# Wide matmuls of a unit ahead of its narrow ones, and values for two pairs of heads in wide matmuls

## The chip, the core and the metric

The kernel runs on one NeuronCore of a Trainium2 chip. What counts is the device time of one execution in microseconds. TensorE (PE) multiplies into PSUM; its weight loads are a row of their own (PEld) and overlap its matmuls. VectorE (DVE), ScalarE (ACT) and GpSimd (POOL) work on SBUF and, the first two, on PSUM; SyncE (SP) issues the DMAs. Each engine takes its instructions in order and waits for the others through semaphores.

## What is computed

Two decoder layers on 256 tokens of width 2048 in float32: latent attention and a convolutional feed-forward (FFN), then dilated attention in three groups and another FFN, each behind an RMS norm and with a residual. In short:

```python
def dilated_mixer(h, positions, w_in, wo):
    qkv = (h @ w_in).reshape(B, S, G, 3, DIL_HEADS, DIL_HEAD_DIM)      # G 3, 16 heads of 128
    for g, (window, dilation) in enumerate(DIL_GROUPS):
        q = partial_rope(qkv[:, :, g, 0], positions)
        k = partial_rope(qkv[:, :, g, 1], positions)
        v = qkv[:, :, g, 2]
        o, l = dilated_group_attention(q, k, v, window, dilation, DIL_HEAD_DIM ** -0.5)
    ...
def conv_ffn(h, w_up, conv_w, conv_b, w_down):                          # hidden 5632
    u = h @ w_up
    ...
    return (jax.nn.silu(gate) * val) @ w_down
def reference(...):
    for i in range(DEPTH):                                              # 2
        h = rms_norm(x, attn_norm[i])
        x = x + (mla_mixer if i % 2 == 0 else dilated_mixer)(h, ...)
        x = x + conv_ffn(rms_norm(x, ffn_norm[i]), ...)
    return rms_norm(x, final_norm)
```

## The kernel before

Activations stand as 16 blocks of 128 features by 256 tokens. Products are made to float32 accuracy from two parts of each factor: ACT copies a factor to the type fp32r (the high part, wh or the left half of xs) and DVE subtracts that copy (the low part, wl or the right half of xs). Three of the four part products count: high by high, high weight by low activation, low weight by high activation.

A **unit** is one output block of 128 features for all tokens. `load` (L68) brings 128 x 2048 weights (1 MB) into one of three staging tiles `w` and splits them, 1024 columns at a time, into wh and wl tiles, of which the pool `wsp` has five each; one unit takes two of each. `proj` (L105) then goes through the 16 blocks k of the sum (14 or 16 in the down projections). For each block it makes a **wide** matmul of 512 columns, wh with both parts of xs, into a whole PSUM bank, and a **narrow** one of 256 columns, wl with the high part, into the bank's right half. In the first block the wide one goes first, in all others the narrow one, so that they alternate:

```python
                def hi():
                    nc.tensor.matmul(ps, wh, xs[k], start=(k == 0), stop=(k == n - 1))

                def lo():
                    nc.tensor.matmul(ps[:, T:], wl, xs[k][:, :T], start=False, stop=False)
                for f in ((hi, lo) if k == 0 else (lo, hi)):
                    f()
```

`joined` (L181) adds the two halves of the bank afterwards: ACT copies the right one to `lo`, DVE adds the left one into `sum`. `unit` (L174) puts down the products of a unit, then one step of attention from the list `steps`, then the evacuation of the unit before; four PSUM banks (`pp`) rotate.

The stages are: the rank projection of the queries (L446 to L460, four banks at once, products as the weights come), the kv ranks, eight pairs of heads of latent attention with short units of 256-column matmuls (`mm3`, L99), the output projection, the first FFN, eight pairs of heads of dilated attention, its output projection, the second FFN, the final norm. An FFN has 88 up units (44 blocks, gate and value) and three down projections of 16 units over 14, 14 and 16 blocks. After an up unit DVE writes `upad`, ACT makes the convolution's first tap `cv` (L724) and DVE the other two (L727), then the gate's product and a split into `a`.

In the dilated stage each pair of heads has 12 units for q and k (three groups, two heads) and 6 for values: `proj_tok` (L123) has 128 tokens as rows and the 2 x 128 columns of a pair as columns, the weights streaming as the moving factor, wide ones with the high and narrow ones with the low part of the activations, alternating as above. `joined_tok` (L189) joins the halves with the norm's factor, and group 0 is split again. Attention's steps of a pair (scores and softmax, two turnings of the probabilities, values, for each of two heads) lie between the units of the next pair.

A scheduler orders each engine's instructions; it may move work between units where its data allow it. The pools set how far: a tile's next writer waits for its last reader.

## Time and profile before

| | us |
|---|---|
| median of 3 runs (2743.19 to 2743.86) | 2743.84 |
| profiled execution, its own time | 2743.58 |
| its span, from first to last instruction | 2741.8 |

| engine | busy us | share of the span | instructions |
|---|---|---|---|
| PE | 2721.1 | 99% | 15964 |
| PEld | 2385.6 | 87% | 15964 |
| DVE | 2016.4 | 74% | 3553 |
| ACT | 1458.2 | 53% | 2305 |
| POOL | 21.5 | 1% | 39 |

Busy time counts a matmul from its start to a modelled end, and matmuls overlap, so PE's share tells that it always has one under way, not how fast they go. For that one reads the distance between starts, which the chain of work prints as the length of its pieces. DMA moves 180 GB/s on average. PE's granted clock stands at nine tenths or more in all 40 slices of the page.

### The profile page before, as it was taken

The page shows a single profiled execution, that of the slowest core. Times are in us where ns is not written, and L with a number is a line of the kernel's source. Part 1 is how long each engine was busy: PE and PEld are TensorE (multiplying, and loading weights), DVE is VectorE, ACT ScalarE, POOL GpSimd, SP SyncE. Part 2 cuts the span into 40 slices and gives each one's busy share as a digit, 9 for nine tenths or more (in the row PEclk, how much of TensorE's full clock was granted, in tenths as well). Part 3 has the DMA queues.
Part 4 walks back from the last instruction along what each step waited for, and adds up shares of the span by engine and source line. Part 5 has one row for each costly group of instructions (what it writes and reads, how often), then busy time and mean ns, then how long its engine had stood idle before and what let it go on. Part 6 is the DMA issues. An engine that isn't in the chain of part 4 may idle for free.

```text
span 2741.8 us, 40682 instructions
## 1 busy us (share of the span) xinstructions
PE 2721.1 (99%) x15964; PEld 2385.6 (87%) x15964; DVE 2016.4 (74%) x3553; ACT 1458.2 (53%) x2305; POOL 21.5 (1%) x39
## 2 busy tenths in 40 slices
PE   8999999999999999999999999999999999999998
PEld 7998888888888888888888888888888888888887
DVE  7987787677678767767767767676778768767775
ACT  6775655455455554545445445454565545545553
POOL 2000000000000000000000000000000000000000
PEclk9999999999999999999999999999999999999999
DMA  6345555555555555454554454544555555555553
GB/s 240 136 142 196 183 189 173 196 185 183 187 198 185 192 185 186 168 185 156 183 185 164 174 174 164 187 158 167 199 184 185 181 192 190 183 185 192 186 187 119
DMA packets 72191, 493.63 MB, mean 180 GB/s; under 512 B 8128, under 2 KB 9280, under 8 KB 21184
## 3 DMA queue, kind: packets, MB, share of 16 engines
q1 hardware_dynamic: 72000, 491.04, 51.8%
q8 instruction: 125, 2.05, 0.3%
q14 instruction: 66, 0.54, 0.1%
HBM read 488.91 MB, written 2.10 MB: 179 GB/s over the span
## 4 chain that ended last, share of the span: by engine, by line
PE 71%; issue 27%; DVE 1%; DMA 0%; ACT 0%; SPq 0%; POOLq 0%; POOL 0%; DVEq 0%; ACTq 0%
PE pp L115 36%; PE pp L118 18%; PE pp L131 7%; PE pp L134 3%; PE pp L101 1%; PE pp L103 1%; PE pp L102 1%; PE po L686 1%; PE ps L655 1%; PE pt L666 1%; DVE xs L233 0%; DMA w<-in_wqa 0%; PE ps L101 0%; PE ps L102 0%; PE ps L103 0%
## 5 line engine op out<-in xcount | busy, mean ns | idle before, releaser
L115 PE MATMUL pp<-xs,wh 128*128 128x512 f32 x4432 | 1554.6, 398 | 0.0
L89 DVE TENSOR_TENSOR wl<-w,wh 128x1024 fp32r<-128x1024 f32 (+2 forms) x843 | 1010.2, 1199 | 318.4 <-ACT wh L88 304.7
L118 PE MATMUL pp<-xs,wl 128*128 128x256 f32 x4432 | 1198.7, 281 | 0.0
L88 ACT ACTIVATE wh<-w 128x1024 fp32r<-128x1024 f32 (+2 forms) x843 | 874.1, 1037 | 604.5 <-PE pp L115 568.5
L115 PEld LDWEIGHTS pp<-xs,wh 128*128 128x128 f32 x4432 | 818.4, 188 | 180.3
L118 PEld LDWEIGHTS pp<-xs,wl 128*128 128x128 f32 x4432 | 837.2, 189 | 22.2
L115 PE MATMUL pp<-a,wh 128*128 128x512 f32 x1920 | 667.9, 397 | 0.0
L118 PE MATMUL pp<-a,wl 128*128 128x256 f32 x1920 | 516.7, 280 | 0.0
L115 PEld LDWEIGHTS pp<-a,wh 128*128 128x128 f32 x1920 | 352.4, 188 | 75.9
L118 PEld LDWEIGHTS pp<-a,wl 128*128 128x128 f32 x1920 | 362.3, 189 | 10.9
L184 ACT ACTIVATE lo<-pp 128x256 f32<-128x256 f32 x273 | 104.1, 381 | 325.9 <-PE pp L115 325.8
L186 DVE TENSOR_TENSOR sum<-pp,lo 128x256 f32<-128x256 f32 x273 | 115.5, 423 | 184.7 <-ACT lo L184 184.7
L727 DVE SCALAR_TENSOR_TENSOR cv<-upad,convs,cv 128x256 f32<-128x256 f32 x352 | 169.1, 482 | 6.1
L131 PE MATMUL pp<-wh,xs 128*128 128x512 f32 x384 | 146.9, 400 | 0.0
L131 PE MATMUL pp<-wl,xs 128*128 128x512 f32 x384 | 144.2, 398 | 0.0
L333 DVE TENSOR_TENSOR x<-x,pp 128x256 f32<-128x256 f32 x256 | 106.8, 420 | 50.7 <-PE pp L115 46.7
L94 ACT ACTIVATE wl<-w 128x512 fp32r<-128x512 f32 x104 | 65.7, 632 | 127.3 <-PE pp L118 127.3
L134 PE MATMUL pp<-wl,xs 128*128 128x256 f32 x384 | 107.8, 281 | 0.0
L724 ACT ACTIVATE cv<-upad,convs 128x256 f32<-128x256 f32 x176 | 105.8, 602 | 0.9 <-DVE upad L721 0.7
L95 DVE TENSOR_TENSOR wl<-w,wl 128x512 fp32r<-128x512 f32 x104 | 71.7, 690 | 42.8 <-ACT wl L94 40.6
L134 PE MATMUL pp<-wh,xs 128*128 128x256 f32 x384 | 99.7, 280 | 0.0
L131 PEld LDWEIGHTS pp<-wl,xs 128*128 128x128 f32 x384 | 72.1, 188 | 17.8
(208 smaller groups left out, 2025.1 us busy)
## 6 DMA issues: line engine op xcount, KB each, us to landing
w<-in_wup SPq DMA_DIRECT2D x176, 1024.0 KB, 4.7
w<-in_win SPq DMA_DIRECT2D x144, 1024.0 KB, 4.8
w<-in_wdn SPq DMA_DIRECT2D x64, 896.0 KB, 4.5
w<-in_wdn SPq DMA_DIRECT2D x32, 1024.0 KB, 4.8
w<-in_wo SPq DMA_DIRECT2D x16, 1024.0 KB, 4.8
w<-in_dwo SPq DMA_DIRECT2D x16, 1024.0 KB, 4.7
w<-in_wkvb SPq DMA_DIRECT2D x8, 1024.0 KB, 4.8
w<-in_wqb SPq DMA_DIRECT2D x8, 768.0 KB, 4.2
```

The costliest lines, as they stand in the source:

```text
L88: nc.scalar.activation(h, w[:, c:e], AF.Copy)
L89: nc.vector.tensor_sub(l, w[:, c:e], h.bitcast(F32))
L95: nc.vector.tensor_sub(t4[:, :, 1, :], src2, t4[:, :, 0, :].bitcast(F32))
L115: nc.tensor.matmul(ps, wh, xs[k], start=(k == 0), stop=(k == n - 1))
L118: nc.tensor.matmul(ps[:, T:], wl, xs[k][:, :T], start=False, stop=False)
L131: nc.tensor.matmul(ps, xs[k][:, tt * P:(tt + 1) * P], w, start=(k == 0), stop=(k == n - 1))
L134: nc.tensor.matmul(ps[:, T:], xs[k][:, T + tt * P:T + (tt + 1) * P], w[:, :T], start=False, stop=False)
L184: nc.scalar.activation(t, ps[:, T:], AF.Copy)
L186: nc.vector.tensor_add(u, ps[:, :T], t)
L333: nc.vector.tensor_add(x, x, a)
L724: nc.scalar.activation(c, u[:, 2:], AF.Identity, scale=convs[:, cw + 2:cw + 3], bias=convs[:, cw + 3:cw + 4])
L727: nc.vector.scalar_tensor_tensor(c, u[:, j:j + T], convs[:, cw + j:cw + j + 1], c, op0=ALU.mult, op1=ALU.add)
```

## The change

- `proj` puts down all wide matmuls of a unit first and then all its narrow ones, and the rank projection of the queries does the same for its four banks in each block.
- Values of the dilated stage are made for two pairs of heads at a time, in every second pair's turn. `load_tok2` brings a quarter of the sum (four blocks) for 2 x 256 columns in two DMAs of 512 KB and splits it so that the 512 columns of a block lie side by side. `proj_tok2` keeps two banks (128 tokens each) open over four quarters and makes all three part products as wide matmuls, added in the bank, so that nothing is left to be joined. Every such quarter is a unit; an even pair's turn has 24 units and an odd one's 12, instead of 18 each.
- `joined_tok` goes; `keep_v` makes one split of 512 columns in group 0 and one copy of 512 in the others, and the value tiles are twice as wide.
- To make room: tiles of `tmp` 4 for 5, of the q and k splits 4 for 5, of probabilities `p` 3 for 4, of `acc` and `sq` (squares for the norms) 1 for 2.
- The second head's scores come one step later.

```diff
-        work = ctx.enter_context(tc.tile_pool(name="work", bufs=5))
+        work = ctx.enter_context(tc.tile_pool(name="work", bufs=4))
...
-            for k in range(since, upto or n):
+            ks = range(since, upto or n)
+
+            def block(k, i):
                 a = k * P
-                wh, wl = (t[:, a % WS:a % WS + P] for t in w[a // WS])
-
-                def hi():
-                    nc.tensor.matmul(ps, wh, xs[k], start=(k == 0), stop=(k == n - 1))
-
-                def lo():
-                    nc.tensor.matmul(ps[:, T:], wl, xs[k][:, :T], start=False, stop=False)
-                for f in ((hi, lo) if k == 0 else (lo, hi)):
-                    f()
+                return w[a // WS][i][:, a % WS:a % WS + P]
+
+            for k in ks:
+                nc.tensor.matmul(ps, block(k, 0), xs[k], start=(k == 0), stop=(k == n - 1))
+            for k in ks:
+                nc.tensor.matmul(ps[:, T:], block(k, 1), xs[k][:, :T], start=False, stop=(k == n - 1),
+                                 skip_group_check=True)
             return ps
...
+        def load_tok2(srcs, q):
+            w = wst.tile([P, D], F32, name="w", tag="w")
+            for i, src in enumerate(srcs):
+                nc.sync.dma_start(w[:, i * WS:(i + 1) * WS], src[q // 2][:, q % 2 * WS:(q % 2 + 1) * WS])
+            w4 = w.rearrange("p (i k c) -> p i k c", i=2, c=T)
+            parts = []
+            for h in range(2):
+                wh = wsp.tile([P, WS], F32R, name="wh", tag="wh")
+                wl = wsp.tile([P, WS], F32R, name="wl", tag="wl")
+                wh4, wl4 = (t.rearrange("p (k i c) -> p i k c", i=2, c=T) for t in (wh, wl))
+                src = w4[:, :, 2 * h:2 * h + 2, :]
+                nc.scalar.activation(wh4, src, AF.Copy)
+                nc.vector.tensor_sub(wl4, src, wh4.bitcast(F32))
+                parts += [(wh[:, ts(k, 512)], wl[:, ts(k, 512)]) for k in range(2)]
+            return parts
+
+        def proj_tok2(w, pss_, xs, q):
+            for k4, (wh, wl) in enumerate(w):
+                k = 4 * q + k4
+                for tt, ps in enumerate(pss_):
+                    xh, xl = xs[k][:, ts(tt, P)], xs[k][:, T + tt * P:T + (tt + 1) * P]
+                    nc.tensor.matmul(ps, xh, wh, start=k == 0, stop=False)
+                    nc.tensor.matmul(ps, xl, wh, start=False, stop=False)
+                    nc.tensor.matmul(ps, xh, wl, start=False, stop=k == KC - 1)
...
-                acc = small.tile([P, T], F32, name="acc", tag="acc", bufs=2)
+                acc = small.tile([P, T], F32, name="acc", tag="acc", bufs=1)
...
-                sq = small.tile([P, T], F32, name="sq", tag="sq", bufs=2)
+                sq = small.tile([P, T], F32, name="sq", tag="sq", bufs=1)
...
-                        h[what] = att.tile([P, 2 * T], F32R, name="qks", tag="qks", bufs=5)
+                        h[what] = att.tile([P, 2 * T], F32R, name="qks", tag="qks", bufs=4)
...
-                        p = att.tile([P, 2 * T], F32, name="p", tag="p", bufs=4)
+                        p = att.tile([P, 2 * T], F32, name="p", tag="p", bufs=3)
...
+                if j % 2 == 0:
+                    state["v"] = {}
+                values = h["v"] = state["v"]
...
+                        if g == 0:
+                            v = att.tile([P, 4 * T], F32R, name="vs", tag="vs", bufs=2)
+                            split((v[:, :2 * T], v[:, 2 * T:]), ps, col)
+                        else:
+                            v = att.tile([P, 2 * T], F32, name="v", tag="v", bufs=4)
+                            nc.scalar.activation(v, ps, AF.Copy, scale=col)
...
+                    if j % 2 == 0:
+                        srcs = [(win_d[b + 4], win_d[b + 5]) for b in (base, base + 6 * NG)]
+                        pss_ = [pp.tile([P, 512], F32, name="pp", tag="pp") for _ in range(2)]
+                        for q in range(4):
+                            w = load_tok2(srcs, q)
+
+                            def quarter():
+                                proj_tok2(w, pss_, xs, q)
+                                return pss_
+
+                            unit(quarter, (lambda p, g=g: keep_v(g, p)) if q == 3 else (lambda p: None))
...
-                (s0, ta0, tb0, v0), (s1, ta1, tb1, v1) = attend(h, 0), attend(h, 1)
+                (s0, ta0, tb0, v0), (s1, ta1, tb1, v1) = (attend(h, e, (j % 2 * 2 + e) * P) for e in range(2))
-                steps.extend([s0, together(ta0, s1), tb0, together(v0, ta1), tb1, v1])
+                steps.extend([s0, ta0, together(tb0, s1), together(v0, ta1), tb1, v1])
```

The first place is PE at the seam of two units of the dilated stage (q or k). Before:

```order
L118 MATMUL pp<-xs_10510,wl 128x256
L115 MATMUL pp<-xs_10510,wh 128x512
L118 MATMUL pp<-xs_10518,wl 128x256
L115 MATMUL pp<-xs_10518,wh 128x512
L115 MATMUL pp<-xs_9795,wh 128x512
L118 MATMUL pp<-xs_9795,wl 128x256
L118 MATMUL pp<-xs_9804,wl 128x256
L115 MATMUL pp<-xs_9804,wh 128x512
```

Now, inside such a unit, where its wide matmuls end and its narrow ones begin:

```order
L117 MATMUL pp<-xs_10408,wh 128x512
L117 MATMUL pp<-xs_10459,wh 128x512
L117 MATMUL pp<-xs_10510,wh 128x512
L117 MATMUL pp<-xs_10518,wh 128x512
L119 MATMUL pp<-xs_9795,wl 128x256
L119 MATMUL pp<-xs_9804,wl 128x256
L119 MATMUL pp<-xs_9898,wl 128x256
L119 MATMUL pp<-xs_9949,wl 128x256
```

The names xs_9795 to xs_10518 are the 16 blocks of activations. Before, a narrow one stands between any two wide ones except at the seam; now there are 16 of a kind in a row.

The second place is PE in the values of the first group (numbers tell tiles apart; pp is a bank). Before:

```order
L131 MATMUL pp_10789<-wh_10763,xs0_9795 128x512
L134 MATMUL pp_10789<-wh_10763,xs0_9795 128x256
L134 MATMUL pp_10789<-wh_10763,xs1_9804 128x256
L131 MATMUL pp_10789<-wh_10763,xs1_9804 128x512
L134 MATMUL pp_10789<-wl_10764,xs2_9898 128x256
L131 MATMUL pp_10789<-wl_10764,xs2_9898 128x512
```

Now:

```order
L147 MATMUL pp_10761<-wh_10766,xs0_9795 128x512
L148 MATMUL pp_10761<-wh_10766,xs0_9795 128x512
L149 MATMUL pp_10761<-wl_10767,xs0_9795 128x512
L147 MATMUL pp_10762<-wh_10766,xs0_9795 128x512
L148 MATMUL pp_10762<-wh_10766,xs0_9795 128x512
L149 MATMUL pp_10762<-wl_10767,xs0_9795 128x512
```

A block had one wide and one narrow matmul in each of two runs through the sum; now it has three wide ones for each of the two banks, one behind the other.

The third place is DVE in the up units of the first FFN. wl is a split of weights (two rows for each w), sum and upad evacuate a bank, cv are the taps. Before:

```order
L89 TENSOR_TENSOR wl_6705<-w_6698,wh_6704 128x1024
L186 TENSOR_TENSOR sum_6687<-pp_6599,lo_6685 128x256
L721 TENSOR_TENSOR upad3_3587<-sum_6687,rb_3685 128x256
L89 TENSOR_TENSOR wl_6754<-w_6751,wh_6753 128x1024
L727 SCALAR_TENSOR_TENSOR cv_6690<-upad3_3587,convs_3579,cv_6690 128x256 x2
L733 TENSOR_TENSOR cv_6690<-cv_6637,cv_6690 128x256
L89 TENSOR_TENSOR wl_6758<-w_6751,wh_6757 128x1024
```

Now:

```order
L89 TENSOR_TENSOR wl_6487<-w_6480,wh_6486 128x1024
L89 TENSOR_TENSOR wl_6536<-w_6533,wh_6535 128x1024
L197 TENSOR_TENSOR sum_6469<-pp_6381,lo_6467 128x256
L740 TENSOR_TENSOR upad3_3587<-sum_6469,rb_3685 128x256
L746 SCALAR_TENSOR_TENSOR cv_6472<-upad3_3587,convs_3579,cv_6472 128x256 x2
L752 TENSOR_TENSOR cv_6472<-cv_6419,cv_6472 128x256
L89 TENSOR_TENSOR wl_6540<-w_6533,wh_6539 128x1024
```

Before, a split stood between upad and the taps, which wait for ACT; now the two splits stand in a row, the second half's of one unit and the first half's of the next, and upad and taps follow each other.

ACT at the same place, with the semaphores that a row waits for. Before:

```order
L184 ACTIVATE lo_6358<-pp_6272 128x256 [waits PE_49,Activation_49]
L88 ACTIVATE wh_6426<-w_6424 128x1024 [waits DMAHW1_49]
L724 ACTIVATE cv_6363<-upad1_3583,convs_3579 128x256 [waits DVE_49]
L88 ACTIVATE wh_6430<-w_6424 128x1024 [waits PE_49,Activation_49]
L319 ACTIVATE a_6368<-cv_6363 128x256 [waits DVE_49]
```

Now:

```order
L195 ACTIVATE lo_6358<-pp_6272 128x256 [waits PE_49,Activation_49]
L88 ACTIVATE wh_6430<-w_6424 128x1024 [waits PE_49]
L743 ACTIVATE cv_6363<-upad1_3583,convs_3579 128x256 [waits DVE_49]
L88 ACTIVATE wh_6482<-w_6480 128x1024 [waits DMAHW2_49,PE_49,Activation_49]
L324 ACTIVATE a_6368<-cv_6363 128x256 [waits DVE_49]
```

The split between lo and cv waited for its DMA before; now the one that stands there waits for PE.

## Rows read from the trace of the kernel before

**Rows 1.** The page's chain that ended last: shares of the span by engine and line

```profile
PE 71%; issue 27%; DVE 1%; DMA 0%; ACT 0%; SPq 0%; POOLq 0%; POOL 0%; DVEq 0%; ACTq 0%
PE pp L115 36%; PE pp L118 18%; PE pp L131 7%; PE pp L134 3%; PE pp L101 1%; PE pp L103 1%; PE pp L102 1%; PE po L686 1%; PE ps L655 1%; PE pt L666 1%; DVE xs L233 0%; DMA w<-in_wqa 0%; PE ps L101 0%; PE ps L102 0%; PE ps L103 0%
```

**Rows 2.** What PE waited for: us in total, times, longest us

```profile
PE pp L459 <- ACT wh L88: 5.8, 1, 5.8
PE pp L459 <- DVE wl L89: 2.6, 2, 2.1
PE po L256 <- ACT last L788: 1.3, 1, 1.3
PE po L263 <- POOL rcol L276: 1.0, 1, 1.0
```

**Rows 3.** The chain in order of time, first FFN: start us, us, what

```profile
598.76 0.46 PE pp L115 x2
...
603.35 0.23 PE pp L115
603.58 0.12 PE pp L118
...
604.05 0.24 PE pp L115
...
604.41 0.46 PE pp L115 x2
604.87 0.23 PE pp L118 x2
...
610.05 0.46 PE pp L115 x2
```

**Rows 4.** One pair of heads, dilated: length, busy us of engines, PEclk, DMA share, GB/s

```profile
1145.34:1254.78 109.44, 109.44 (x651) 96.17 (x650) 77.38 (x156) 53.21 (x87) 0.00 (x0) 1.00 0.49 173
```

**Rows 5.** The chain in order of time, latent attention, a run of 256-column matmuls

```profile
99.99 0.12 PE pp L101
...
101.04 0.12 PE pp L101
```

**Rows 6.** Groups by line: count, then busy us and mean ns

```profile
L115 PE MATMUL pp<-xs,wh 128*128 128x512 f32 x4432 | 1554.6, 398 | 0.0
...
L115 PE MATMUL pp<-a,wh 128*128 128x512 f32 x1920 | 667.9, 397 | 0.0
...
L131 PE MATMUL pp<-wh,xs 128*128 128x512 f32 x384 | 146.9, 400 | 0.0
L131 PE MATMUL pp<-wl,xs 128*128 128x512 f32 x384 | 144.2, 398 | 0.0
```

**Rows 7.** The longest pieces of the chain: starts of units of 14 pairs

```profile
457.59 0.47 PE pp L115 x2
462.44 0.46 PE pp L115 x2
467.38 0.47 PE pp L115 x2
```

**Rows 8.** Timeline of the first stage, ACT, POOL and PE: start us, us, instruction

```profile
10.48 0.40 ACT L227 ACTIVATE sq<-x 128x256 f32<-128x256 f32 x1
...
22.91 4.92 POOL L228 TENSOR_TENSOR acc<-acc,sq 128x256 f32<-128x256 f32 x4 [0.53 <-ACT sq L227]
...
36.01 0.50 PE L254 MATMUL po<-ones,acc 128*128 128x1 f32 x4
```

**Rows 9.** Timeline of an up unit, ACT and DVE: start us, us, instruction

```profile
605.02 1.06 ACT L88 ACTIVATE wh<-w 128x1024 fp32r<-128x1024 f32 x1
605.15 0.42 DVE L186 TENSOR_TENSOR sum<-pp,lo 128x256 f32<-128x256 f32 x1 [0.59 <-ACT lo L184]
605.61 0.43 DVE L721 TENSOR_TENSOR upad<-sum,rb 128x256 f32<-128x256 f32 x1
606.08 0.60 ACT L724 ACTIVATE cv<-upad,convs 128x256 f32<-128x256 f32 x1
606.11 1.22 DVE L89 TENSOR_TENSOR wl<-w,wh 128x1024 fp32r<-128x1024 f32 x1
607.25 1.00 DVE L727 SCALAR_TENSOR_TENSOR cv<-upad,convs,cv 128x256 f32<-128x256 f32 x2
```

More of the change, by code (lines that the diff above doesn't have):

```diff
@@ L121, in proj @@
-            return ps
-        def proj_tok(pieces, xs, tt):
-            ps = pp.tile([P, 512], F32, name="pp", tag="pp")
-            n = 4 * len(pieces)
-            for k in range(n):
-                w = pieces[k // 4][k % 4 // 2][:, k % 2 * 2 * T:(k % 2 + 1) * 2 * T]
-                def hi():
-                    nc.tensor.matmul(ps, xs[k][:, tt * P:(tt + 1) * P], w, start=(k == 0), stop=(k == n - 1))
-                def lo():
-                    nc.tensor.matmul(ps[:, T:], xs[k][:, T + tt * P:T + (tt + 1) * P], w[:, :T],
-                                     start=False, stop=False)
-                for f in ((hi, lo) if k == 0 else (lo, hi)):
-                    f()
-            return ps
+                return w[a // WS][i][:, a % WS:a % WS + P]
@@ L187, in joined @@
             return u
-        def joined_tok(dst, ps, col):
-            t = work.tile([P, T], F32, name="lo", tag="lo", bufs=2)
-            nc.scalar.activation(t, ps[:, T:], AF.Copy, scale=col)
-            nc.vector.scalar_tensor_tensor(dst, ps[:, :T], col, t, op0=ALU.mult, op1=ALU.add)
         ones = const.tile([P, 1], F32, name="ones")
@@ L454, in mla @@
                 wh, wl = w[k % 4 // 2]
-                for b in range(RC):
-                    c = k % 2 * RANK + b * P
-                    mms = [(banks[b], wh[:, c:c + P], xs[k]), (banks[b][:, T:], wl[:, c:c + P], xs[k][:, :T])]
-                    for i, (o, l, r) in enumerate(mms if k == 0 else mms[::-1]):
-                        nc.tensor.matmul(o, l, r, start=(k == 0 and i == 0), stop=(k == KC - 1 and i == 1))
+                for i, t in enumerate((wh, wl)):
+                    for b in range(RC):
+                        c = k % 2 * RANK + b * P
+                        nc.tensor.matmul(banks[b][:, i * T:], t[:, c:c + P], xs[k][:, :(2 - i) * T],
+                                         start=(k == 0 and i == 0), stop=(k == KC - 1),
+                                         skip_group_check=i == 1)
                 squares(xt[k], k, "x", nc.gpsimd)
@@ L624, in keep_qk, with keep_v @@
                         h[what] = t
-                def keep_v(g, tt, ps):
-                    if g == 0:
-                        v = work.tile([P, T], F32, name="v0", tag="tmp")
-                    else:
-                        v = att.tile([P, T], F32, name="v", tag="v", bufs=4)
-                    joined_tok(v, ps, tabs["r"][:, tt:tt + 1])
-                    h["v", g, tt] = v
-                    if g == 0:
-                        h["v", g, tt] = att.tile([P, 2 * T], F32R, name="vs", tag="vs", bufs=2)
-                        split_to(h["v", g, tt], v)
+                if j % 2 == 0:
+                    state["v"] = {}
+                values = h["v"] = state["v"]
+                def keep_v(g, pss_):
+                    for tt, ps in enumerate(pss_):
+                        col = tabs["r"][:, tt:tt + 1]
+                        if g == 0:
[4 more added lines that the diff above has]
+                            nc.scalar.activation(v, ps, AF.Copy, scale=col)
+                        values[g, tt] = v
                 for g in range(NG):
@@ L642, in project, with attend @@
                             unit(lambda: proj(w, xs, KC), lambda ps, what=what, g=g, e=e: keep_qk((what, g, e), ps))
-                    w = load(win_d[base + 4], D) + load(win_d[base + 5], D)
-                    for tt in range(2):
-                        unit(lambda: proj_tok(w, xs, tt), lambda ps, g=g, tt=tt: keep_v(g, tt, ps))
+                    if j % 2 == 0:
[7 more added lines that the diff above has]
+                            unit(quarter, (lambda p, g=g: keep_v(g, p)) if q == 3 else (lambda p: None))
                 return h
-            def attend(h, e):
+            def attend(h, e, c):
                 def scores():
@@ L685, in values @@
                         for t in range(2):
-                            nc.tensor.matmul(po[:, ts(t, P)], h["v", g, t][:, ts(e, P)],
+                            nc.tensor.matmul(po[:, ts(t, P)], h["v"][g, t][:, c:c + P],
                                              pt[:, ts(2 * (g - 1) + t, P)], start=False, stop=False)
@@ L780, in trunk_kernel @@
             dilated()
-        last = small.tile([P, T], F32, name="last", tag="sq", bufs=2)
+        last = small.tile([P, T], F32, name="last", tag="sq", bufs=1)
         def final(c):
```

4 lines of the change are left out of this document (2 added, 2 removed).

## The prediction

> **What bounds the kernel now.** The chain of work that ended last comes first: 71% of it is PE, nearly all on four lines of matmuls, L115, L118, L131 and L134, and the 27% called issue lie between the starts of matmuls [rows 1]. Next the rows on what PE waited for: 10.7 us in the whole span, 8.4 of them in the first stage [rows 2]. So after the first stage nothing but the pace of matmuls sets the time, and it is read from their starts, as the ends are modelled. The chain in order of time prints that pace: inside a unit a 512-column matmul takes 0.23 to 0.24 us, a 256-column one 0.12, and three pairs repeat: 603.35 to 604.41, 1.06 us, 0.353 a pair [rows 3]. The granted clock is 1.00, the 2.4 GHz level [rows 4]; nothing is to be won or lost there.
>
> Where one unit ends and the next begins, the kernel before already does for one pair what the change does for all: its last matmul and the next unit's first both have 512 columns, the two after them 256. These rows read 0.46 for the two wide ones and 0.23 for the two narrow ones [rows 3]: 0.345 a pair where alternation takes 0.353. A second way gives the same: from one such place to the next stand 16 pairs, 15 of them alternating, in 5.645 us (598.76, 604.41, 610.05; mean of 5.65 and 5.64) [rows 3]; 5.645 - 15 x 0.3533 = 0.345. And a long run of 256 columns with a load of weights before each stands in the latent attention: nine from 99.99 to 101.04, 0.117 each [rows 5]. That leaves 0.345 - 0.117 = **0.228 us for a 512-column matmul in a run**. No row shows a run of more than two of these, so on this number all hangs.
>
> **The change part by part.** *Units of 16 pairs.* L115 runs 4432 times on xs and 1920 times on a [rows 6]. On xs that is 277 units of 16 (5 of the kv rank, 96 of q and k, 176 of the FFN's up); on a 32 of the two output projections, and 64 of 14 and 32 of 16 in the down projections. So 341 units of 16 and 64 of 14. The order of PE's instructions keeps the runs whole, with attention's steps between units. A unit of 16 becomes 16 x 0.345 = 5.52; saved 0.125, 341 times, **42.6 us**.
> *Units of 14* take 4.85 and 4.94 by turns (457.59, 462.44, 467.38) [rows 7], 4.895 on average; 14 x 0.345 = 4.83; saved 0.065, 64 times, **4.2 us**. Those of 4.85 are at 0.346 a pair while still alternating: the alternation has two rhythms, and the slow one has the units of 16 shown.
> *Dilated values.* 768 wide matmuls, in two rows of 384 [rows 6], and as many narrow ones go: 48 units at the alternating 5.645, 271.0 us. They become 4 pairs of head pairs x 3 groups x 16 blocks x 2 token halves x 3 = 1152 wide ones and no narrow one. The columns are equal (589,824 either way), the instructions a quarter fewer. 1152 x 0.228 = 262.7; saved **8.3 us**. The loads bring the same bytes in 48 more DMAs on SP; three staging tiles hide them, and PE's waits show that no unit waits for a load now [rows 2]. Without that cover a unit would stand until its second half MB has landed. ACT and DVE lose work there, off the path.
> *First stage.* With one buffer for squares, ACT's square waits for POOL's addition of the last one: 0.40 + 1.23 (4 in 4.92) [rows 8], 15 times from 10.48, ends at 34.9, or at 38 with 0.2 us of handing over each time. PE reaches the sum of squares at 36.01 and would wait there: 0 to 2 us, I take **1 us lost**. Wide matmuls may also start there before wl is done; of PE's 2.6 us behind wl [rows 2] some may come back, which I don't count.
> *Buffers* of tmp (5 to 4), q and k splits (5 to 4), p (4 to 3): the shortest cover is that of a q split, whose tile the scores free up to two units into the next pair of heads; ACT and DVE then stand for part of a unit while PE has weights for two more: nothing. Without the cover it would be up to half a unit of 5.5 us in each of 8 pairs, 22 us. The second head's scores come one step later, with a unit between them and their use either way: nothing.
> *DVE in the FFN's up units.* Here the change adds a wait. The wl tile of a unit's first half is now read until 5/6 of the unit, before until 1/2; DVE's next split into that tile waits for it, behind it stands the next evacuation, and for that waits ACT's convolution. DVE's row per unit by the order: two splits at a spacing of 1.14 (606.11 to 607.25), sum to upad 0.46, upad 0.43, ACT's cv (0.04 after its end, 0.60 long), two taps 1.00, a product of upad's size 0.43, and 0.05 of handing over: 5.3 us [rows 9] against 5.52. It fits with 0.2 to spare, and PE has weights for two units, so it sees nothing. But it is a floor: up units can't go below 5.3.
> Sum: 42.6 + 4.2 + 8.3 - 1 = 54 us, from the profiled 2743.58 (span 2741.8 and 1.8 around it, 0.3 below the median of the runs): **2690 us**.
>
> *Bounds of the one price.* Slowest: a wide matmul in a run keeps what it takes in the alternation, 0.353 - 0.117 = 0.236. Fastest by rows: at 2.4 GHz the 0.117 of rows 5 are 280 cycles, 24 more than columns; were that a surcharge per matmul, a wide one would take 536 cycles, 0.223. I stay at 0.228, which both places with a wide pair give. At 0.223 (0.340 a pair) the saving is 69.9 + 8.6 + 14.1 - 1 = 92: 2652. At 0.233 (0.350) it is 15.3 - 0.3 + 2.6 - 1 = 17: 2727.
>
> Rows 5 have a load before each narrow matmul and 0.117 for the two together; in rows 3 a narrow one takes 0.12 while the load of the next, wide one goes on. With 0.117 the sum is as above. A rule speaks against grouping here: by the Trainium skill, "TensorE: Matmul & The Clock Gate", section "LDWEIGHTS (loading the stationary operand)", a load takes its columns at 1.2 GHz, 107 ns for 128, which is as long as 256 columns stream at 2.4 GHz; in a run of narrow ones no load has slack, and each hand-over shows. An estimate by it, with 3 ns more for each of 6352 narrow matmuls, is 19 us less saved, 2709; rows 5 already contain such a run, so I go by them.
>
> **The rivals.** *Wide runs at the pace of columns alone.* If all that a wide matmul takes over its columns at 2.4 GHz (0.213 us) comes from narrow neighbours, the pair is 0.330. For: no wide one with wide ones on both sides was ever seen. Against: rows 3 have two in 0.46, not 0.43. The up units stop at DVE's 5.3: 176 x 0.345 + 165 x 0.365 + 64 x 0.275 + 25 = 163 saved, **2580**. (The Trainium skill, same page, section "Back-to-back issue gap", has N/2.4 + 2.5 ns for isolated matmuls, 216 and 109 ns; rows 5 are 8 ns above it.)
> *No gain.* The cost is per column (0.236 and 0.117 are two to one), and the shorter boundary is only a rhythm out of step. For: the fast rhythm of rows 7 needs no grouping. Against: the unit's sum gives 0.345 a second time. Then **2744**, within 0.2%.
> *DVE becomes the bound in the up units.* In ACT's order cv stands behind a wh split that now waits for PE's first eight wide matmuls, 1.8 us into a unit. If that lands in DVE's row each time, 1.06 us more [rows 9], the row is 6.35: 176 x 0.705 = 124 lost, 33 gained elsewhere, **2835**. It decides from 5.83 on (176 x 0.185 = 33). Against: cv then starts 2.9 us into the unit, and by the row above DVE is at splits, sum and upad until about 2.7; the wait lies beside work.
> *The runs are not there*: the scheduler could have mixed them again. Its order shows that it hasn't; **2744**.
>
> **How the numbers follow.** Forecast (2652 to 2727) 0.70; columns alone 0.07; no gain 0.13; DVE's bound 0.08; runs not there 0.02. The likeliest is 2690. The range goes from 2640 to 2745: it takes in no gain, and leaves out DVE's bound and columns alone, under 0.2 with the forecast's own edges. About 0.2%, 5.5 us, is what a measurement of this kernel can tell from no change. Faster: 0.70 + 0.07 + 0.02 of the cases near no gain = 0.79; same: 0.12, most of those; slower: 0.08 + 0.01 of them = 0.09.
>
> **What would show it.** In the chain, 16 wide in 3.65 us and 16 narrow in 1.87; unit starts 5.52 apart in q and k, FFN and output projections alike; the three wide ones of a block of values in 0.68; two pairs of heads, 2 x 109.44 now [rows 4], shorter by 5 us; PE's waits still near 11 us. Wide runs at 0.236 make the forecast wrong by the price; a list of PE's waits for wl, or up units longer than q and k units, make it wrong by DVE; a first stage that ends over 2 us later, by POOL.

## The result and the profile after

The changed kernel takes **2711.34 us** (median of 4 runs, 2710.98 to 2712.63); the kernel before took 2743.52 beside it (2742.53 to 2743.86). The ratio is 0.9884, 95% interval 0.9867 to 0.9901: 32 us faster, where 54 were forecast. The profiled execution took 2712.63 us, its span is 2710.9. The sums below are made against the spans, 2741.8 and 2710.9, which differ by 30.9.

The page's chain of the kernel after, shares of the span by engine and by line, answers to [rows 1]:

```profile
PE 70%; issue 27%; DVE 0%; POOL 0%; POOLq 0%; DVEq 0%
PE pp L117 35%; PE pp L119 18%; PE pp L147 3%; PE pp L148 3%; PE pp L149 3%; PE pp L101 1%; PE pp L103 1%; PE pp L102 1%; PE po L705 1%; PE pt L685 1%; PE ps L674 1%; PE ps L101 0%; PE ps L103 0%; PE ps L102 0%; PE pt L569 0%
```

L117 is now the wide matmul of `proj`, L119 the narrow one, L147 to L149 the three of a block of values. The bound is what it was: the pace of matmuls. What PE waited for in the kernel after (us in total, times, longest us), to be read against [rows 2]:

```profile
PE pp L463 <- ACT wh L88: 8.7, 4, 5.8
PE pp L117 <- DVE rank L411: 1.4, 1, 1.4
PE po L261 <- ACT last L807: 1.3, 1, 1.3
PE po L268 <- POOL rcol L281: 1.0, 1, 1.0
PE po L268 <- DVE rb L273: 0.8, 1, 0.8
PE po L268 <- DVE s L294: 0.3, 1, 0.3
```

They add up to 13.5 us after 10.7, and no wait of the FFN's or the dilated units for weights is among them. The pace stands in the chain in order of time (start us, us, what), first FFN, as [rows 3]:

```profile
601.00 1.91 PE pp L119 x16
602.92 3.65 PE pp L117 x16
606.57 1.91 PE pp L119 x16
608.48 3.65 PE pp L117 x16
```

A run of matmuls now prints as one piece. A unit of 16 is 3.65 + 1.91, from 602.92 to 608.48: 5.56 us (5.566 to the ns), after 5.645 before and with 5.52 forecast. The units of 14 in the down projections, as [rows 7]:

```profile
457.45 3.20 PE pp L117 x14
460.65 1.67 PE pp L119 x14
462.32 3.20 PE pp L117 x14
```

That is 4.87 us, after 4.895, with 4.83 forecast. A block of values takes 0.68 us from one L147 to the next, as forecast; the chain of the kernel after in the dilated stage:

```profile
1040.10 0.23 PE pp L147
1040.32 0.23 PE pp L148
...
1040.78 0.23 PE pp L147
```

Where the time came from is told by windows over the same stages in both kernels: first FFN, dilated attention with its output projection, second FFN, and two pairs of heads out of the dilated stage. The columns are the stretch, its length, busy us of PE, PEld, DVE, ACT and POOL with their instructions, the granted clock, DMA's share, GB/s. Of the kernel before:

```profile
276.87:1021.53 744.66, 744.66 (x4234) 647.39 (x4232) 558.41 (x841) 403.58 (x569) 0.69 (x1) 1.00 0.55 188
1021.53:1988.85 967.32, 967.27 (x5706) 848.80 (x5705) 684.07 (x1348) 472.26 (x753) 0.89 (x5) 1.00 0.50 175
1988.85:2727.86 739.01, 739.01 (x4202) 642.44 (x4201) 544.05 (x816) 397.58 (x561) 0.69 (x1) 1.00 0.53 181
1145.18:1364.06 218.88, 218.88 (x1299) 192.35 (x1297) 154.74 (x312) 106.43 (x173) 0.00 (x0) 1.00 0.49 173
```

Of the kernel after:

```profile
279.65:1015.51 735.86, 735.86 (x4235) 650.21 (x4234) 535.71 (x842) 402.65 (x569) 1.61 (x1) 1.00 0.56 190
1015.51:1967.96 952.45, 952.45 (x5323) 833.24 (x5321) 660.11 (x1197) 459.79 (x617) 1.81 (x5) 1.00 0.51 177
1967.96:2697.50 729.54, 729.54 (x4200) 644.80 (x4198) 521.94 (x817) 395.03 (x560) 1.61 (x1) 1.00 0.54 183
1168.97:1384.38 215.41, 215.41 (x1202) 188.44 (x1201) 149.37 (x275) 103.40 (x139) 0.00 (x0) 1.00 0.51 176
```

The granted clock is 1.00, the 2.4 GHz level, in all of them. The windows shrink by 8.8, 14.9 and 9.5 us, and the two pairs of heads by 3.5, where 5 were forecast. Ahead of them 3.2 us are lost by the start of the latent attention (66.01 before, 69.19 after) and 0.4 won back until the first FFN; the end gains 0.5. Together 30.9. The windows begin where PE sums the squares of a norm. In the kernel after, three wide matmuls of the next stage's first unit (0.7 us) stand ahead of that place, and none stand ahead of the last norm; with them counted where they belong, the second FFN gains 8.8 like the first, and the latent stage 1.1. Within the dilated stage, the distances between starts of matmuls, summed by line, split its 14.9 us: the units of 16 (q, k and the output projection, 112 of them) go from 632.8 to 626.6 us, the values from 271.6 to 262.2, attention's own steps from 62.9 to 63.6.

So the gain by the prediction's own terms:

| term | forecast, us | measured, us |
|---|---|---|
| units of 16 and of 14 | 42.6 + 4.2 | 24.9 (8.8 in each FFN, 6.2 in the dilated stage, 1.1 in the latent one with its other steps) |
| values | 8.3 | 9.4 |
| first stage | -1 | -3.2 |
| attention's steps, the end | 0 | -0.7 + 0.5 |

### The profile page after: what moved, and what is told of

Its sections match the earlier page's. It is cut to its first block, busy times and chain, and to the rows that moved or that the text cites. A ratio compares the mean times of both kernels' runs of the same rounds, so it can differ in the third digit from the quotient of the medians.

```text
span 2710.9 us, 39595 instructions
## 1 busy us (share of the span) xinstructions
PE 2688.4 (99%) x15580; PEld 2376.1 (88%) x15580; DVE 1941.7 (72%) x3401; ACT 1443.2 (53%) x2169; POOL 27.5 (1%) x39
## 4 chain that ended last, share of the span: by engine, by line
PE 70%; issue 27%; DVE 0%; POOL 0%; POOLq 0%; DVEq 0%
PE pp L117 35%; PE pp L119 18%; PE pp L147 3%; PE pp L148 3%; PE pp L149 3%; PE pp L101 1%; PE pp L103 1%; PE pp L102 1%; PE po L705 1%; PE pt L685 1%; PE ps L674 1%; PE ps L101 0%; PE ps L103 0%; PE ps L102 0%; PE pt L569 0%
## 5 line engine op out<-in xcount | busy, mean ns | idle before, releaser
L117 PE MATMUL pp<-xs,wh 128*128 128x512 f32 x4432 | 1060.7, 391 | 1.4 <-DVE rank L411 1.4
L117 PEld LDWEIGHTS pp<-xs,wh 128*128 128x128 f32 x4432 | 814.7, 188 | 160.7 <-DVE rank L411 1.5
L119 PEld LDWEIGHTS pp<-xs,wl 128*128 128x128 f32 x4432 | 568.2, 191 | 21.5
L119 PE MATMUL pp<-xs,wl 128*128 128x256 f32 x4432 | 574.9, 283 | 0.0
L117 PE MATMUL pp<-a,wh 128*128 128x512 f32 x1920 | 462.5, 391 | 0.0
L117 PEld LDWEIGHTS pp<-a,wh 128*128 128x128 f32 x1920 | 351.6, 188 | 67.1
L119 PEld LDWEIGHTS pp<-a,wl 128*128 128x128 f32 x1920 | 248.5, 191 | 10.5
L119 PE MATMUL pp<-a,wl 128*128 128x256 f32 x1920 | 252.3, 283 | 0.0
L136 ACT ACTIVATE wh<-w 128x1024 fp32r<-128x1024 f32 x96 | 101.7, 1059 | 109.2 <-PE pp L148 58.4
L137 DVE TENSOR_TENSOR wl<-w,wh 128x1024 fp32r<-128x1024 f32 x96 | 115.5, 1222 | 59.6 <-ACT wh L136 38.6
L147 PE MATMUL pp<-wh,xs 128*128 128x512 f32 x384 | 150.2, 391 | 0.0
L148 PE MATMUL pp<-wh,xs 128*128 128x512 f32 x384 | 149.5, 389 | 0.0
L149 PE MATMUL pp<-wl,xs 128*128 128x512 f32 x384 | 149.5, 389 | 0.0
L149 PEld LDWEIGHTS pp<-wl,xs 128*128 128x128 f32 x384 | 72.1, 188 | 15.2
L147 PEld LDWEIGHTS pp<-wh,xs 128*128 128x128 f32 x384 | 72.1, 188 | 14.5
```

The source lines that it names most:

```text
L117: nc.tensor.matmul(ps, block(k, 0), xs[k], start=(k == 0), stop=(k == n - 1))
L119: nc.tensor.matmul(ps[:, T:], block(k, 1), xs[k][:, :T], start=False, stop=(k == n - 1), skip_group_check=True)
L137: nc.vector.tensor_sub(wl4, src, wh4.bitcast(F32))
L147: nc.tensor.matmul(ps, xh, wh, start=k == 0, stop=False)
L148: nc.tensor.matmul(ps, xl, wh, start=False, stop=False)
L149: nc.tensor.matmul(ps, xh, wl, start=False, stop=k == KC - 1)
```

## The experiments

All kernels here compute the whole reference. The theory: the order inside a unit makes the gain, through the price of a matmul in a run; values come on top. Distances between starts, to the ns, showed what that price is after the change: 227 ns for a wide matmul in a run, 120 for a narrow one, and about 20 ns more for each unit, because the first five wide matmuls after a narrow run take 233, 236, 228, 233 and 231 (27 ns over) and the first two narrow ones 113 and 119 (8 under). What had to be told apart: how much is due to each part; whether the alternation before was slow by its nature or by the swap in its first block; whether the 20 ns are a price of the seam or one that the narrow matmuls of a run build up; and why a narrow one takes 0.120 and not the 0.117 of [rows 5].

### Each part alone

`e1_proj` is the kernel before with the new `proj` only (and the rank projection still alternating):

```diff
...
-                for f in ((hi, lo) if k == 0 else (lo, hi)):
-                    f()
...
+            for k in ks:
+                nc.tensor.matmul(ps, block(k, 0), xs[k], start=(k == 0), stop=(k == n - 1))
+            for k in ks:
+                nc.tensor.matmul(ps[:, T:], block(k, 1), xs[k][:, :T], start=False, stop=(k == n - 1),
+                                 skip_group_check=True)
```

> The kernel before with the grouped order in the projections alone; values, buffers, the first stage's order and the attention steps as before. Pace theory (in a run a wide matmul takes 0.2268 us and a narrow one 0.120, a unit of 16 pairs 5.566 instead of 5.645 with 27 ns lost where wide follow narrow): 341 x 0.079 + 64 x 0.022 = 28 us less than before, 2715, and the first stage ends where it ended before. Rival (the changed kernel owes most of its 32 us to the values): 10 to 15 us less, about 2730.

Measured: 2718.47 us, ratio 0.9908 (0.9893 to 0.9922): 25.2 us less than the 2743.70 of the kernel before in those runs, 3 short of the 28 expected.

`e2_values` is the kernel after with the old, alternating `proj` (the same lines the other way round).

> The changed kernel with the projections alternating again; values for two pairs, fewer buffers and the grouped rank projection stay. Pace theory: values save 48 units of 5.645 less 1152 x 0.2268 = 9.7 us, the start loses 3, the seams of attention up to 3: 2737 to 2740. Rival (values carry the gain): 2720 to 2725.

Measured: 2736.51 us, ratio 0.9975 (0.9965 to 0.9985): 7.2 less. The two parts add up to 32.4, the whole gain, so the two don't work on each other to speak of.

### Is the alternation slow by its nature?

The kernel before swaps the order in the first block of a unit, so that two wide matmuls meet at each boundary. `e3_hi_lo` is the kernel before without that swap:

```diff
...
-                for f in ((hi, lo) if k == 0 else (lo, hi)):
-                    f()
+                hi()
+                lo()
```

> The kernel before with wide, narrow in every block, so that two wide or two narrow ones never meet; nothing else is changed. Theory that the slow rhythm (0.353 a pair, three pairs 1.060) belongs to alternation as such: all units alternate without the shorter seam, 404 x 0.007 to 0.010 = 3 to 4 us more, 2747. Rival (the seam kicks alternation into the slow rhythm, and left alone it keeps the fast one of 0.3465): units of 16 take 5.545, 341 x 0.100 + 64 x 0.044 = 37 us less, 2707, which would be as good as grouping.

Measured: 2744.97 us, ratio 1.0005 (0.9995 to 1.0014): no change by the interval. The chain of this kernel in order of time, wide matmuls in the first FFN:

```profile
600.13 0.24 PE pp L115
...
600.50 0.23 PE pp L115
...
600.85 0.23 PE pp L115
...
601.20 0.24 PE pp L115
```

Three pairs in 1.07 us, the slow rhythm again, now without a seam anywhere. But the unchanged total hides two changes that cancel. The windows of this kernel over the first FFN, the dilated stage with its output projection and the second FFN, to be read against those of the kernel before:

```profile
276.95:1023.97 747.02, 747.02 (x4234) 648.02 (x4233) 554.11 (x841) 389.35 (x569) 0.69 (x1) 1.00 0.55 187
1023.97:1986.06 962.09, 962.05 (x5707) 848.37 (x5705) 685.12 (x1348) 472.71 (x753) 0.89 (x5) 1.00 0.50 176
1986.06:2727.52 741.46, 741.46 (x4203) 643.16 (x4202) 539.45 (x816) 384.04 (x561) 0.69 (x1) 1.00 0.53 181
```

Each FFN takes 2.4 us more than in the kernel before, the dilated stage 5.2 less. The units that begin behind the values step of attention (L103), four on end with each pair of heads and the last fifteen of the output projection, alternate in the fast rhythm. The chain there:

```profile
1919.32 0.23 PE pp L115
...
1924.86 0.23 PE pp L115
```

Sixteen pairs in 5.54 us, 0.346 each. To the ns 43 of the stage's 112 units take 5.547, less than the 5.566 of a unit in runs; the same fifteen take 5.64 in the kernel before. So each theory is half right. Alternation isn't slow by its nature: left alone it kept the rhythm that it started with in these stretches, and the seam of the kernel before did throw it out of the fast one. But in the FFNs it started in the slow one and stayed there. The runs gain because their 5.566 holds in the FFNs too. What chooses the rhythm, and whether alternation could be kept in the fast one through the FFNs (the expectation has 2707 for that), wasn't tried.

### What a seam costs

`e6_runs4` is the kernel after with runs of 4 wide and 4 narrow matmuls, four seams in a unit for one:

```diff
-            for k in ks:
-                nc.tensor.matmul(ps, block(k, 0), ...)
-            for k in ks:
-                nc.tensor.matmul(ps[:, T:], block(k, 1), ...)
+            for c in range(0, len(ks), 4):
+                for k in ks[c:c + 4]:
+                    nc.tensor.matmul(ps, block(k, 0), ...)
+                for k in ks[c:c + 4]:
+                    nc.tensor.matmul(ps[:, T:], block(k, 1), ...)
```

> The changed kernel with runs of 4 wide and 4 narrow in the projections instead of 16 and 16. If wide ones after narrow ones cost 27 ns at each seam whatever the run: a unit has four seams instead of one, 3 x 20 ns net more, 341 x 0.060 + 64 x 0.055 = 24 us more than the changed kernel, 2735. If it is a debt that grows with the number of narrow ones (16 narrow cost 27, 4 cost 7): a unit as it is, 2711.

Measured: 2726.24 us, ratio 0.9935 (0.992 to 0.995), 15 us more than the kernel after and between the two theories. Its chain in order of time, first FFN:

```profile
601.04 0.47 PE pp L120 x4
601.51 0.93 PE pp L118 x4
602.44 0.48 PE pp L120 x4
602.92 0.93 PE pp L118 x4
```

Four wide ones take 0.93, not 4 x 0.227 = 0.91; four narrow ones 0.47 and 0.48 by turns. Two groups of four and four, from 601.04 to 603.85, take 2.81 us where eight pairs in long runs would take 8 x 0.3468 = 2.77: 17 ns for each seam (the mean over some 1480 such groups, 1.404 us, gives the same), after 20 behind 16 narrow ones. A unit has four of these, 68 ns for 20, or 405 x 0.048 = 19 us in all. From the start of the latent attention to the end this kernel takes 15.6 us more than the kernel after (2657.3 from 67.43 on, 2641.7 from 69.19 on); the rest of the 19 isn't accounted for. So it is mostly a price of the seam, a little smaller behind a short run.

`e7_snake` is the kernel after with every second unit turned, narrow matmuls first, so that runs of 32 arise where no attention step lies between units:

```diff
...
+            turn[0] = not turn[0] if ks[0] == 0 and ks[-1] == n - 1 else False
+            a, b = (wide, narrow) if turn[0] or ks[0] or ks[-1] < n - 1 else (narrow, wide)
+            a(True)
+            b(False)
```

> The changed kernel with every second unit of a projection turned round (narrow first, then wide), so that runs are of 32 and there are half as many seams; the same matmuls. Fixed cost at a seam: 20 ns net less for each two units, 200 x 0.020 = 4 us less than the changed kernel, 2707. Debt that grows with the narrow ones: no change, 2711. If the wl of a unit, now needed at its start, comes too late: waits of PE for it and more time.

Measured: 2706.49 us, ratio 0.9866 (0.9851 to 0.988): 4.9 us less than the kernel after, with 4 forecast. By the profiles 4.3 us lie behind the start of the latent attention (2637.4 us from there on, after 2641.7), and 2.5 ahead of it, in the first stage (below). Its chain in order of time:

```profile
596.19 7.28 PE pp L120 x32
603.47 3.83 PE pp L125 x32
607.30 7.28 PE pp L120 x32
```

32 wide ones take 7.28 us: 32 x 0.2267 and once 0.027. A run twice as long, behind one twice as long, pays the same, once: the price belongs to the seam. What in the chip makes it, no run shows.

### Why a narrow matmul takes 0.120 us

Four kernels ask this. `e5_left` is the kernel after with the narrow matmuls in the left half of the bank, where the latent attention's go:

```diff
-                nc.tensor.matmul(ps[:, T:], block(k, 1), xs[k][:, :T], ...
+                nc.tensor.matmul(ps[:, :T], block(k, 1), xs[k][:, :T], ...
```

> The changed kernel, but narrow matmuls add into the left half of the bank instead of the right one (the halves are summed afterwards). Theory that a matmul in a run pays a fixed 32 cycles over its columns: nothing moves, 2711. Rival (the latent attention's 0.117 for a narrow one against 0.120 here comes from the half that is written): 6352 x 0.0033 = 21 us less, 2690.

Measured: 2712.05 us, ratio 0.9885 (0.9871 to 0.99), as the kernel after; its chain in the first FFN has

```profile
600.38 1.91 PE pp L119 x16
```

still 0.120 each. `e9_no_same_weights` and `e10_no_same_moving` change the order of `mm3` in the kernel after, so that in the latent attention no neighbours share their weights, or none their moving factor:

```diff
 # e9_no_same_weights
-            nc.tensor.matmul(ps, al, bh, ...)
-            nc.tensor.matmul(ps, ah, bh, ...)
+            nc.tensor.matmul(ps, ah, bh, ...)
+            nc.tensor.matmul(ps, al, bh, ...)
             nc.tensor.matmul(ps, ah, bl, ...)
 # e10_no_same_moving
             nc.tensor.matmul(ps, al, bh, ...)
-            nc.tensor.matmul(ps, ah, bh, ...)
             nc.tensor.matmul(ps, ah, bl, ...)
+            nc.tensor.matmul(ps, ah, bh, ...)
```

> In the kernel after, mm3 puts down ah by bh, al by bh, ah by bl, so that no 256-column matmul of the latent attention has the weights of the one before it (now the last two of three share ah); the first two still share the moving factor. What is told apart is why a 256-column matmul takes 0.117 us there and 0.120 in the narrow run of a unit, where weights and moving factor change with every matmul. If shared weights are the cause, steady stretches of the latent attention's units go from 116.7 to 120 ns a matmul; if the shared moving factor is, or something of the place (the stage, its other engines), they stay at 116.7. The whole time stays within 3 us of the kernel after either way (650 such matmuls by 3 ns are 2 us).

> In the kernel after, mm3 puts down al by bh, ah by bl, ah by bh, so that the last two of three share the weights as now, but no two neighbours share the moving factor. If the shared moving factor is what makes 0.117 us of 0.120, steady stretches of the latent attention's units go from 116.7 to 120 ns; if shared weights or the place are, they stay at 116.7. With both this and the other order at 116.7 the place is left; with both at 120 each of the two sharings is needed. The whole time stays within 3 us of the kernel after.

Measured: 2712.04 and 2712.20 us (one execution each). The chain in the latent attention of the first:

```profile
103.31 0.12 PE pp L101
...
104.36 0.12 PE pp L101
```

Nine matmuls in 1.05 us, 0.117 each; and of the second, six in 0.70, 0.117 again:

```profile
102.75 0.12 PE pp L101
...
103.45 0.12 PE pp L101
```

Neither sharing makes the difference, nor would either do by itself: in the first of the two, two of three neighbours share nothing, and in the steady stretch they take 116 and 117 ns all the same. `e11_two_tiles` is the kernel after with the blocks of a unit taken from its two tiles of weights by turns:

```diff
+            ks = sorted(ks, key=lambda k: (k * P % WS, k))
...
             for k in ks:
                 nc.tensor.matmul(ps, block(k, 0), xs[k], ...)
...
```

> The kernel after, with the blocks of a unit taken from its two tiles of weights by turns (0, 8, 1, 9, ...; the order of the sum changes, nothing else), in the wide run and in the narrow one. In the latent attention neighbouring 256-column matmuls take weights from different tiles mostly (al, then ah twice), in the narrow run of a unit all eight neighbours take them from one tile, block behind block. If that is why a narrow matmul takes 0.120 us in a unit and 0.117 there, the narrow run goes to 0.117 (and the wide run from 0.227 perhaps to 0.223), a unit of 16 loses 0.05 (to 0.11) us, and the time falls by 20 us (to 44) from 2711. If it is not, the gaps stay at 227 and 120 and the time within 3 us. A loss would come from the tiles' release: the wide run then needs the second half of the weights at once, and both tiles of wl are read until the unit's end, which shows in PE's waits for wh or wl.

Measured: 2710.81 us, ratio 0.9882 (0.9866 to 0.9899), as the kernel after, and in its chain

```profile
601.00 3.65 PE pp L119 x16
604.66 1.91 PE pp L121 x16
```

nothing has moved. The half of the bank, shared weights, a shared moving factor and the tile of weights are out. In `e7_snake`, narrow runs that follow an attention step directly take 119.3 to 119.9 ns a matmul from the third on, so a wide run ahead of them isn't needed either. What is left, the stage itself and what runs beside it, wasn't tried: the cause stays open.

### The first stage

`e4_squares2` is the kernel after with two buffers again for squares and their sum, out of a pool that is otherwise idle then, in the first stage only:

```diff
-                acc = small.tile([P, T], F32, name="acc", tag="acc", bufs=1)
+                acc = (own or small).tile([P, T], F32, name="acc", tag="acc", bufs=2 if own else 1)
...
-                sq = small.tile([P, T], F32, name="sq", tag="sq", bufs=1)
+                sq = (own or small).tile([P, T], F32, name="sq", tag="sq", bufs=2 if own else 1)
```

> The changed kernel with two buffers again for squares and their sum in the first stages, nothing else. Theory that one buffer costs what the start loses (the second sum of squares at 50.05 us against 47.76, latent attention 3.2 us later): it comes back, 2708. Rival (the grouped order of the rank projection or of the kv units costs it): 2711, the start as in the changed kernel.

Measured: 2709.58 us, ratio 0.9876 (0.9859 to 0.9892): 1.8 us less by the medians, and its slowest run (2710.20) is below the fastest of the kernel after (2710.98); by the profiled spans 2.9 less (2708.0 and 2710.9). The timeline of the first stage (start us, us, instruction), POOL's last sum and PE around its sum of squares, in the kernel after:

```profile
35.16 0.74 POOL L233 TENSOR_TENSOR acc<-acc,sq 128x256 f32<-128x256 f32 x1 [0.53 <-ACT sq L232]
```

```profile
36.40 0.63 PE L463 MATMUL pp<-xs,wl 128*128 128x256 f32 x4
36.87 0.50 PE L259 MATMUL po<-ones,acc 128*128 128x1 f32 x4
38.82 0.50 PE L117 MATMUL pp<-xs,wh 128*128 128x512 f32 x1 [1.45 <-DVE rank L411]
```

and with two buffers:

```profile
28.15 0.83 POOL L233 TENSOR_TENSOR acc<-acc,sq 128x256 f32<-128x256 f32 x1 [0.45 <-ACT sq L232]
```

```profile
34.90 0.50 PE L259 MATMUL po<-ones,acc 128*128 128x1 f32 x4
35.64 3.68 PE L117 MATMUL pp<-xs,wh 128*128 128x512 f32 x15 [0.24 <-DVE rank L411]
```

PE doesn't wait for the sum of squares: POOL has ended at 35.90, and PE comes to it at 36.87 straight from its matmuls. Its wait stands behind it, 1.45 us until DVE has evacuated the ranks (L411, the results of the rank projection). That wait is 1.4 to 1.5 us in all eight kernels here with one buffer and at most 0.2 in the five with two, whatever the order inside units. It is what one buffer costs.

The latent attention starts at 66.00 with two buffers, at 69.19 in the kernel after and at 66.01 in the kernel before. Of the 3.2 us between the last two, 0.9 arise until the first sum of squares (36.01 to 36.87), 1.4 from there to the second (11.75 and 13.18 us), and 0.9 behind it (18.25 and 19.14).
- The first 0.9 aren't shown to be the change's. Kernels with one buffer reach that place between 34.74 (`e2_values`) and 36.87, those with two between 34.90 and 36.01. The granted clock differs as well: it was 0.50, the 1.2 GHz level, for 3.41 us in the profile of the kernel after (13.89 to 17.30; PE had been busy for 1.62 of the 3.89 us from 10.00 on) and in that of the kernel before (14.99 to 18.40), and 1.00 up to that place in `e2_values`, `e4_squares2` and `e7_snake`. So the 2.0 us between 36.87 and 34.90 aren't all the buffer's either.
- The 1.4 are the wait for the ranks.
- The last 0.9 aren't the buffers'. PE waits 0.8 us there for `rb`, a copy on DVE (L273). It does so in `e1_proj` and `e4_squares2` too, which have two buffers, and not in `e7_snake` and `e11_two_tiles`, which have one: it goes with the order of the units.

`e8_both` joins `e7_snake` and `e4_squares2`.

> Turned units and two buffers for squares together. If both theories hold: 3 + 4 us less than the changed kernel, 2704, faster than both kernels. If only one does: 2707 or 2708.

Measured: **2705.64 us**, ratio 0.9861 (0.9847 to 0.9876), faster than both kernels by the medians, and 1.6 us above what was expected: it is 0.85 us below `e7_snake`, where the two buffers were to give 3. `e7_snake` starts its latent attention at 66.74 with one buffer, this kernel at 65.10, so there was less to win than the 3.2 of the kernel after.

## Why the prediction came out so

**The bound and the mechanism were right.** PE's pace was the bound and still is; runs are faster than the alternation in its slow rhythm, and `e1_proj` shows that they alone give 25 of the 32 us. The price on which all was said to hang came out: 0.228 us was forecast for a wide matmul in a run, 0.227 measured, and the 1152 of the values took 262.2 us after a forecast of 262.7. That it came out so near was luck. The rows print hundredths of a us; to the ns, the two wide ones at the boundary of [rows 3] take 236 and 227 and the two narrow ones 113 and 119, 0.3475 a pair, and the same working then gives 0.3475 - 0.117 = 0.2305.

**The step that failed is the price of a pair**, "0.345 a pair" in units of 16 and 14. The term was forecast at 46.8 us and measured at 24.9. The gain that was sought is 0.008 us a pair, and the rows from which it was read step by 0.010. The boundary pair is 0.3475 (0.348 on average over 346 such places of the kernel before), and with that the prediction's own working gives 341 x 0.085 + 64 x 0.03 = 31 us. The second way couldn't tell the two apart: 1.06 us for three pairs is good to 5 ns, and fifteen pairs of it to 25. How a pair in runs comes to its 0.348 is another matter; three parts differ from the forecast.
- *The narrow price.* 0.117 came from a run in the latent attention [rows 5]. In a unit a narrow matmul takes 0.120 (1.91 for 16). The 3 ns are small, but stand 16 times in a unit: 0.048 of the 0.125 us that a unit was to save. The boundary pair seemed to bear 0.117 out with 0.23 for two narrow ones, but the first of them is short (113 ns), as it is behind a run of 16 wide ones.
- *The seam.* A run of 16 wide ones behind a narrow run takes 3.65, 0.027 more than 16 x 0.2267. The 8 ns that the narrow run wins off, 20 ns a unit remain, 7 us over 341. `e7_snake` takes about half of these away.
- *The wide price*, 0.2267 for 0.228, gives 0.021 of a unit back.

With all three, a unit takes 5.566 and saves 0.079: 341 x 0.079 + 64 x 0.022 = 28.3 us, 18.5 short of the forecast. The units of the dilated stage fall short even of that (6.2 us for 112, 0.055 each): a unit by itself behind an attention step takes 5.65 to 5.66 us, after 5.64 to 5.68 before, and so gains little (its wide run is 3.68 instead of 3.65 in the chain, 1170.82 to 1174.50). The five units of the kv rank lie in the first stage, which gained nothing.

The prediction named a rule that speaks against grouping: by the Trainium skill, "TensorE: Matmul & The Clock Gate", section "LDWEIGHTS (loading the stationary operand)", a load takes its columns divided by 1.2 in ns. For 128 columns that works out at 107 ns, as long as 256 columns stream at 2.4 GHz, so that a load in a narrow run would have no slack. No run here times a load by itself, and that each hand-over then shows is the prediction's own inference. Its estimate with 3 ns more for each narrow matmul, 2709 us, came out nearer to the 2711 measured than the sum did, but in part by luck: the 3 ns fit, yet the estimate has neither the seam nor the short gain in the dilated stage, and the wide price made up for some of them. That the load is the cause no run here shows: weights shared by neighbours or not, and one tile or two, changed nothing.

**The first stage** was forecast to lose 1 us to the one buffer for squares. The buffer costs 1.4, near enough in size, but not by the step that was named: PE was to wait at the sum of squares for POOL, and it doesn't wait there; it waits behind it for the ranks. The profiles show 3.2 us lost in all. The wait for `rb` was no term of the sum, and the rest is within what executions differ by at that place. The prediction's "nothing is to be won or lost" by the clock was read from a stretch of the dilated stage [rows 4]; in the first stage 3.41 us of the kernel before ran at a granted 0.50.

**The rivals.** *Columns alone* (0.213 us a wide matmul) is out: 0.227, in runs of 32 too. *No gain* is out by the interval; but its ground, that the fast rhythm needs no grouping, is borne out by the units of 5.547 us in `e3_hi_lo`. *DVE as the bound in the up units* is out as a bound, but its mechanism is there. Two groups of the page after, DVE's splits and the taps of the convolution (busy us, mean ns | idle us before them, releaser):

```profile
L89 DVE TENSOR_TENSOR wl<-w,wh 128x1024 fp32r<-128x1024 f32 (+2 forms) x843 | 995.5, 1195 | 390.7 <-PE pp L119 280.4
L746 DVE SCALAR_TENSOR_TENSOR cv<-upad,convs,cv 128x256 f32<-128x256 f32 x352 | 170.7, 485 | 183.8 <-ACT cv L743 177.6
```

DVE's splits now wait 280 us in all for narrow runs to release their tiles, and its taps 178 us for ACT's first tap, 6 before. PE doesn't see it: among its waits stands no wl, and up units take 5.56 like the others. The prediction's reason, that the wait lies beside work, holds. The buffers of tmp, q and k splits and p, costed at nothing, show in no wait of PE.

## What to carry to other kernels

A difference of 8 ns can't be read from rows that step by 10. The place was well chosen here, as the boundary pair to the ns (0.348) is what a pair took in runs; the rounded row said 0.345, and that 1% of a unit was over a third of what it was to save. Price a run from a run where there is one: a run of another stage had 0.117 for 0.120. Grouping matmuls of one width gave 25 us of 2744 where PE's pace is the bound; turning every second unit, so that equal runs meet, gave about 4 more. A total that doesn't move can hide two changes that cancel, as in `e3_hi_lo`: look at the stages before a theory is dropped. And when a stage loses time, find where PE waits before giving the loss to the buffer that was cut: of 3.2 us here, 1.4 were the buffer's.

## What the runs showed of the hardware

- In a run, with a load of weights before each, a 512-column matmul took 226.7 ns and a 256-column one 120.0: at the granted 2.4 GHz that is 544 and 288 cycles, 32 over the columns in both. In the latent attention steady runs of 256 columns took 116.7 ns, 280 cycles. Which of the two holds where stays open.
- Strict alternation of the two widths has two rhythms, 0.353 and 0.347 us a pair, against 0.348 in units with runs. Left alone it kept one of them: in `e3_hi_lo` the slow one through both FFNs, the fast one through fifteen units of the output projection. What chooses it no run shows.
- After a run of 16 or 32 narrow matmuls the first five wide ones together take 27 ns more, at either length.
- The granted clock was 0.50 for 3.41 us of the first stage in the profiles of the kernels before and after, and 1.00 there in `e2_values`, `e4_squares2` and `e7_snake`.
